# An fp32 transformer trunk on one core: a third K pair of the MLP's up projections as seven block products

## The chip, the cores and the metric

The kernel runs on one core of a Trainium2 chip. The metric is device time in microseconds, the median of three runs of the whole program.

## What is computed

A trunk of two decoder layers on 256 tokens of width 2048, all in float32: an attention of one kind in the first layer, of another in the second, and in each layer an MLP and a gated per-layer embedding. The change is in the MLP:

```python
hn = rmsnorm(h, mlp_norm_g[i])
h = h + jnp.square(jax.nn.relu(hn @ mlp_w1[i])) @ mlp_w2[i]
```

`mlp_w1[i]` is 2048 x 8192 and `mlp_w2[i]` 8192 x 2048, so that there are 33.6 million weights for the MLP of a layer, for 256 tokens.

## The kernel before

**The products.** A float32 matrix is used as two parts, a high one that TensorE's fp32r takes exactly and a low one, the rest. A product has three matmuls: high by high, low by high, high by low (`terms`). Weights come as chunks of 128 x 1024 floats: two K tiles (128 rows each) by 512 features. ScalarE copies a raw chunk to its high part (`copy`, L243, tile whi), VectorE subtracts to get the low one (`sub`, L251, wlo), and TensorE takes both. The features of 512 columns are called a quad. A quad over K = 2048 has eight chunks (K pairs), of 24 matmuls for a K pair of two quads, 12 for each chunk: two K tiles, two halves of the tokens (128 each), three matmuls. The tokens' part stands still in the array (`xa`, or `h` in the downs) and the weights stream through, 512 columns a matmul.

**The order of work.** `Program.run` goes through a list of chunks. At chunk n it emits the loads up to n + 7 as far as the four raw buffers allow, the copies up to n + 4, the splits up to n + 3, then one piece each of the work that goes on beside (generators, `advance`), and then the matmuls of chunk n. Each engine takes its instructions in the order in which they are emitted. There are six buffers for high parts and five for low ones.

**The MLP** (`mlp`) goes in four blocks of 2048 features. A block has four quads of ups (`up_plain`, `up_mixed`) and then four quads of downs over the same features (`downs`). The first two quads of a layer are plain. The other ups go in pairs of quads, seven in each layer: one pair in the first block, two in each of the other three. "First pair of a layer", "early pair" (right after the downs of the block before) and "late pair" (right after the early one) are used below.

**A pair** (`up_mixed`, `pair_major`) shares the chunks of two quads. Six of the eight K pairs are plain. The other two (MIXED = (2, 5)) are taken as a product of 2 x 2 blocks (tokens' halves by K tiles, K tiles by quads) in seven block products in place of eight, 21 matmuls for 24. For that VectorE makes two further weight chunks: t, a sum of the first quad's chunk a and a half of the second quad's chunk b (`make_t`, L531, tile ts), and u, two sums of half a chunk, written over b (`make_u`, L536 and L537). So a mixed K pair is a set of four chunks a, b, t and u with 6, 3, 6 and 6 matmuls, of which a, t and u are split in full and b by half. The raw chunk of a is held until u is made. The sums of the tokens' blocks, the forms (tile xf), are made once a layer by `x_forms`, after the two plain quads. The chunks stand in the order

```
first quad 0, 1 | set 2 | first quad 3, second quad 0, first quad 4 | set 5 | first quad 6, 7 | second quad 1, 3, 4, 6, 7
```

**What follows a pair.** After the last set four sums (`sums`, L778 to L783) make the common part of both quads' results; the banks' own part is added to it when a quad's last chunk is through (`done`, L790), ScalarE takes ReLU (L792) and square (L749), VectorE transposes blocks (L697), the rows go out to a DRAM tile (dU, L196) and come back turned, in four transfers (L200), and ScalarE and VectorE split them into high and low parts h (L757, L759), half a quad at a time. All this is spread over the chunks that come after. The second quad of a pair ends with the pair, so for an early pair it falls into the late pair, and for a late pair into the downs.

Of the kernel before, what the change touches and what calls it, by code (L numbers as in the profile page):

```python
# [10 lines left out]
F32 = mybir.dt.float32  # L11
F32R = mybir.dt.float32r
# [22 lines left out]
DMA_AHEAD = 7  # L35
SPLIT_AHEAD = 3
RAW_BUFS, HI_BUFS, LO_BUFS = 4, 6, 5
MIXED = (2, 5)

G_ATTN, G_MLP, G_PLE, G_KV, G_FIN = 0, 2, 4, 6, 7  # L40

# [1 line left out]
def f32(ap):  # L43
    return ap.bitcast(F32)
# [116 lines left out]
def kernel(ctx: ExitStack, tc: tile.TileContext, a: dict, out: bass.AP):  # L161
# [386 lines left out]
    def x_forms(k, gi, to):  # L548


        u = [tmp.tile([P, T], F32, tag="sq", name="sq", bufs=3) for _ in range(3)]
        for i in range(2):
            nc.scalar.activation(u[i], x[k + i], AF.Identity, scale=gain(gi, k + i))
        yield
        a, b, s = u
        nc.vector.tensor_sub(s[:, :P], a[:, P:], b[:, P:])
        nc.vector.tensor_sub(s[:, P:], a[:, :P], a[:, P:])
        nc.vector.tensor_sub(a[:, :P], a[:, :P], s[:, :P])
        nc.vector.tensor_sub(b[:, :P], b[:, :P], a[:, :P])
        f = cur["z"].tile([P, 2, 2 * T], F32R, tag="xf", name="xf", bufs=2)  # L560
        parts = ((slice(0, T), s), (slice(T, T + P), a[:, :P]), (slice(T + P, 2 * T), b[:, :P]))
        for c, v in parts:
            nc.scalar.copy(f[:, 0, c], v)
        yield
        for c, v in parts:
            nc.vector.tensor_sub(f[:, 1, c], v, f32(f[:, 0, c]))
        to[k // 2] = f
# [29 lines left out]
    def to_head(ps, norm, dst, roped, mark, late=0, lo=None):  # L597

        t = sum_halves(ps)
        for _ in range(1 + late):  # L600
            yield
        while norm.r is None:
            yield
        if callable(dst):
            dst = dst()
        elif dst is None:
            dst = t
        if not roped:
            nc.vector.tensor_mul(dst, t, norm.rb)
        else:  # L610
            sh = tmp.tile([32, T], F32, tag="rsh", name="rsh", bufs=2)
            nc.vector.stream_shuffle(sh, t[:32, :], ROPE_SWAP)
            nc.vector.tensor_mul(dst, t, norm.rc)
            nc.vector.tensor_mul(sh, sh, norm.rs)
            nc.vector.tensor_add(dst[:32, :], dst[:32, :], sh)
        if lo is not None:
            yield
            nc.scalar.copy(lo[0], dst)
            yield
            nc.vector.tensor_sub(lo[1], dst, f32(lo[0]))  # L620
        mark()
# [19 lines left out]
            out[-1].append(s)  # L641
        return out

    def taken_late(f, g, ops=()):

        both = [by_chunk(prog.collect(p)) for p in (f, g)]
        for c in range(0, KT // 2, 2):
            if c == KT // 2 - 2:
                for fn in ops:
                    prog.op(fn)  # L650
            for steps in both:
                prog.steps += steps[c] + steps[c + 1]

    def out_proj(src, nk, oT, gi, to, norm, hooks, twos, close):

# [70 lines left out]
    def mlp(layer, xg, norm, to, norm2, opening):  # L726
# [20 lines left out]
        def up(b, q, t):  # L747

            nc.scalar.activation(t, t, AF.Square)  # L749
            yield  # L750
            yield
            w = yield from turned(t, second if b == 0 and q == 1 else new)
            w4 = w.rearrange("p a (n i j r) -> p n a (i j) r", n=2, i=2, r=32)
            for n in range(2):
                h = cur["z"].tile([P, 2, 2, T], F32R, tag="h", name="h", bufs=8)
                h5 = h.rearrange("p c i (j a r) -> p c a (i j) r", j=2, r=32)
                nc.scalar.copy(h5[:, 0], w4[:, n])  # L757
                yield
                nc.vector.tensor_sub(h5[:, 1], w4[:, n], f32(h5[:, 0]))  # L759
                for i in range(2):  # L760
                    hid[b][4 * q + 2 * n + i] = (h[:, 0, i], h[:, 1, i])

        def up_plain(b, q, ps0, ps1, mm):

# [7 lines left out]
        def up_mixed(b, q):  # L772

            ts = []

            def sums(aux):
                s, o = row(), row()
                nc.scalar.copy(s[:, 0], aux["P1"])  # L778
                yield
                nc.vector.tensor_sub(s[:, 1], aux["R6"], s[:, 0])  # L780
                nc.vector.tensor_add(o[:, 0], aux["Q5"], s[:, 1])
                nc.vector.tensor_sub(s[:, 1], aux["Q7"], s[:, 1])
                nc.vector.tensor_sub(o[:, 1], o[:, 0], aux["Q7"])  # L783
                ts.extend((s, o))

            def done(i, ps):
                while not ts:
                    yield
                t = ts[i]
                nc.vector.tensor_add(t, ps, t)  # L790
                for j in range(2):
                    nc.scalar.activation(t[:, j], t[:, j], AF.Relu, scale=norm.col[:, j:j + 1])  # L792
                yield from up(b, q + i, t)

            plain_ = [c for c in range(KT // 2) if c not in MIXED]
            c0, c1, c2, c3, c4, c5 = plain_
            order = [(0, c0), (0, c1), MIXED[:1], (0, c2), (1, c0), (0, c3), MIXED[1:], (0, c4), (0, c5)] + \
                [(1, c) for c in plain_[1:]]
            pair_major(lambda i, c: a["w1"][layer * 128 + (b * 4 + q + i) * 8 + c], order, xg, forms, sums, done)

        def normed(k):
# [24 lines left out]
        def downs(b, q):  # L826
            token_major(chunks("w2", b, q), hid[b], lambda *ps: down(b, q, *ps), whole=True)

        taken_late(lambda: ups(0, 0, {4: [lambda: norm.factor(rows=True)]}), lambda: ups(0, 1), opening)
        def all_forms():  # L830
            for c in MIXED:
                yield from x_forms(2 * c, G_MLP + layer, forms)
                yield
        prog.op(all_forms)
        for b in range(NFB):
            for q in range(0, 4, 2):
                if b or q:
# [536 lines left out]
    def key_unit(n, i, which, at, hooks=None):  # L1374

        def done(ps0, ps1, mm):
# [3 lines left out]
            for g in range(GB):  # L1380
                while n_b1.r is None:
                    yield
                k4, c4, s4 = (v.rearrange("p (j a r) -> p j a r", j=2, a=4) for v in
                              (cur["E"].tile([P, T], F32, tag="et", name="et", bufs=7), n_b1.rc, n_b1.rs))
                src = w.rearrange("p a (g j r) -> p g j a r", j=2, r=32)[:, g]
                sh = tmp.tile([32, T], F32, tag="rsh", name="rsh", bufs=2)
                sh4 = sh.rearrange("p (j a r) -> p j a r", j=2, a=4)
                nc.vector.tensor_mul(k4, src, c4)
                nc.vector.stream_shuffle(sh4, src[:32], ROPE_SWAP)
                nc.vector.tensor_mul(sh4, sh4, s4)  # L1390
                nc.vector.tensor_add(k4[:32], k4[:32], sh4)
                yield
                t2 = k4.rearrange("p j a r -> p j (a r)")
                nc.scalar.copy(kt_blocks(g, 0, which), t2)
                yield
                nc.vector.tensor_sub(kt_blocks(g, 1, which), t2, f32(kt_blocks(g, 0, which)))
# [208 lines left out]

    def q_done(h, ps):
        t = sum_halves(ps)
        sh = tmp.tile([32, T], F32, tag="rsh", name="rsh", bufs=2)
        nc.vector.stream_shuffle(sh, t[:32, :], ROPE_SWAP)
        nc.vector.tensor_mul(t, t, n_b1.rc)  # L1610
        nc.vector.tensor_mul(sh, sh, n_b1.rs)
# [245 lines left out]
```

## Time and profile before

| | |
|---|---|
| Time, median of three runs | 2447.5 us (2447.45 to 2448.7) |
| Time of the profiled execution | 2447.25 us |
| Its span | 2445.5 us |
| Granted TensorE clock | 0.999 |
| TensorE, VectorE, ScalarE busy | 100%, 73%, 56% of the span |
| HBM | 217 GB/s over the span |

A busy time counts an engine's instructions, not how full they keep it; matmuls are pipelined. What ended an engine's idle time stands behind an arrow in the rows of the profile; "PE" is TensorE, "DVE" VectorE, "ACT" ScalarE, "SPq" the queue of SyncE, which issues the loads. Names are those of the program's tiles: mm and at are PSUM banks.

### The profile page before, as it was taken

How to read it: one execution, taken by the hardware profiler on the slowest of the kernel's cores; microseconds unless marked ns; L12 is line 12 of the kernel's file. 1: busy time of each engine (PE TensorE's matmuls, PEld its weight loads, DVE VectorE, ACT ScalarE, POOL GpSimd, SP SyncE). 2: the span in 40 equal slices, each digit the busy share in tenths (PEclk: the TensorE clock that was granted, in tenths of full speed). 3: DMA queues.
4: the chain of work that ended last, by engine and by line, in shares of the span. 5: the costliest groups of instructions: out<-in, count | busy, mean ns of one | idle time of the engine just before them, and what ended most of it. 6: DMA issues, size and time to landing. Idle time of an engine off the chain costs nothing.

```text
span 2445.5 us, 33009 instructions
## 1 busy us (share of the span) xinstructions
PE 2434.5 (100%) x11763; PEld 2050.8 (84%) x11763; DVE 1774.0 (73%) x2666; ACT 1371.5 (56%) x1997; POOL 10.3 (0%) x24
## 2 busy tenths in 40 slices
PE   9999999999999999999999999999999999999998
PEld 8888888888888888888888889988888888888887
DVE  7866687776585675777678989867658668567766
ACT  6544444565464454564564788756545546445556
POOL 0000000000000000000100000000000000000000
PEclk9999999999999999999999999999999999999999
DMA  7666665767577576687776743476857757758775
GB/s 276 201 214 215 196 210 197 223 222 249 182 240 235 190 250 220 194 271 241 243 242 210 256 165 121 141 226 219 262 182 233 240 186 239 233 187 257 247 233 161
DMA packets 174981, 532.26 MB, mean 218 GB/s; under 512 B 19616, under 2 KB 51808, under 8 KB 174816
## 3 DMA queue, kind: packets, MB, share of 16 engines
q1 hardware_dynamic: 173712, 528.30, 66.3%
q8 instruction: 92, 1.51, 0.2%
q0 software_dynamic: 528, 1.07, 0.1%
q10 hardware_dynamic: 576, 0.79, 0.1%
q14 instruction: 73, 0.60, 0.1%
HBM read 496.00 MB, written 34.08 MB: 217 GB/s over the span
## 4 chain that ended last, share of the span: by engine, by line
PE 99%; DVE 0%; DMA 0%; ACT 0%; SPq 0%; issue 0%; ACTq 0%; DVEq 0%
PE at L589 26%; PE mm L589 25%; PE at L493 21%; PE mm L384 11%; PE mm L386 6%; PE mm L493 3%; PE at L384 1%; PE at L386 1%; PE at L1682 1%; PE mm L1706 0%; PE mm L1446 0%; PE mm L916 0%; PE mm L918 0%; PE mm L917 0%; PE mm L1447 0%; PE at L1167 0%
## 5 line engine op out<-in xcount | busy, mean ns | idle before, releaser
L251 DVE TENSOR_TENSOR wlo<-raw,whi 128x1024 fp32r<-128x1024 f32 (+1 forms) x903 | 1075.8, 1199 | 500.3 <-PE mm L589 151.3
L243 ACT CAST whi<-raw 128x1024 fp32r<-128x1024 f32 (+1 forms) x903 | 930.5, 1039 | 727.2 <-PE mm L589 207.6
L493 PE MATMUL at<-whi,xa 128*128 128x512 f32 x1456 | 448.2, 389 | 0.0
L384 PE MATMUL mm<-xa,whi 128*128 128x512 f32 x1104 | 371.7, 395 | 0.0
L493 PEld LDWEIGHTS at<-whi,xa 128*128 128x128 f32 x1456 | 273.3, 188 | 56.8
L589 PE MATMUL mm<-whi,h 128*128 128x512 f32 x1024 | 315.2, 389 | 0.0
L589 PE MATMUL at<-whi,h 128*128 128x512 f32 x1024 | 315.2, 389 | 0.0
L493 PE MATMUL at<-wlo,xa 128*128 128x512 f32 x728 | 283.2, 389 | 0.0
L386 PE MATMUL mm<-xa,wlo 128*128 128x256 f32 x1104 | 273.3, 278 | 0.0
L589 PEld LDWEIGHTS at<-whi,h 128*128 128x128 f32 x1024 | 192.2, 188 | 39.9
L589 PEld LDWEIGHTS mm<-whi,h 128*128 128x128 f32 x1024 | 192.2, 188 | 39.9
L386 PEld LDWEIGHTS mm<-xa,wlo 128*128 128x128 f32 x1104 | 207.3, 188 | 18.0
L384 PEld LDWEIGHTS mm<-xa,whi 128*128 128x128 f32 x1104 | 193.3, 188 | 30.5 <-issue 0.4
L589 PE MATMUL at<-whi,xa 128*128 128x512 f32 x672 | 208.0, 391 | 1.5 <-DVE et L392 1.3
L589 PE MATMUL mm<-whi,xa 128*128 128x512 f32 x656 | 202.8, 390 | 0.0
L589 PE MATMUL mm<-wlo,h 128*128 128x512 f32 x512 | 199.2, 389 | 0.0
L589 PE MATMUL at<-wlo,h 128*128 128x512 f32 x512 | 199.2, 389 | 0.0
L493 PEld LDWEIGHTS at<-wlo,xa 128*128 128x128 f32 x728 | 136.6, 188 | 28.3
L589 PEld LDWEIGHTS at<-whi,xa 128*128 128x128 f32 x672 | 125.2, 189 | 26.9 <-issue 1.4
L589 PEld LDWEIGHTS mm<-whi,xa 128*128 128x128 f32 x656 | 122.5, 188 | 25.1
L589 PE MATMUL at<-wlo,xa 128*128 128x512 f32 x336 | 130.6, 390 | 0.2 <-DVE wlo L251 0.2
L589 PE MATMUL mm<-wlo,xa 128*128 128x512 f32 x328 | 127.7, 389 | 0.0
(405 smaller groups left out, 2698.5 us busy)
## 6 DMA issues: line engine op xcount, KB each, us to landing
raw<-in_w SPq DMA_DIRECT2D x512, 512.0 KB, 4.4
raw<-in_w_qk SPq DMA_DIRECT2D x96, 512.0 KB, 3.7
raw<-in_w_gate SPq DMA_DIRECT2D x64, 512.0 KB, 4.3
raw<-in_w_kv SPq DMA_DIRECT2D x48, 512.0 KB, 4.4
raw<-in_w_v SPq DMA_DIRECT2D x47, 512.0 KB, 4.4
dU<-z SPq DMA_DIRECT2D x46, 512.0 KB, 4.2
w<-dU SPq DMA_DIRECT2D x184, 128.0 KB, 5.0
raw<-in_w_q SPq DMA_DIRECT2D x32, 512.0 KB, 4.2
```

The lines of the kernel that those rows point to most:

```text
L243: nc.scalar.copy(hi[:, c], t[:, c])
L251: nc.vector.tensor_sub(lo[:, c], t[:, c], f32(hi)[:, c])
L384: nc.tensor.matmul(ps, hi[:, col:col + P], rhs, start=first, stop=False)
L386: nc.tensor.matmul(ps[:, :T], lo[:, col:col + P], rhs[:, :T], start=False, stop=last)
L493: nc.tensor.matmul(ps, x_, w_, start=b not in touched, stop=end and last[b] == n and i == 2)
L589: nc.tensor.matmul(st[j], *parts[j][i], start=k == i == 0, stop=k == kt - 1 and i == 2)
L1682: nc.tensor.transpose(tr[:, i * P:(i + 1) * P], src, ident)
```

## The change

MIXED becomes (1, 3, 5): three K pairs as sets, with a third buffer for forms. The order of a pair's chunks becomes

```
first quad 0, 2 | set 1 | first quad 4 | set 3 | first quad 6 | set 5 | first quad 7 | second quad 0, 2, 4, 6, 7
```

The layout of w1 in DRAM follows MIXED by itself. The forms are now made in the last plain chunks, before the second plain quad's last two (`mid` of `taken_late`). A quad's 512 features are split into h in one instruction each on ScalarE and VectorE, in place of two (lines L760 and L762 of the new kernel), with four buffers of four K tiles in place of eight of two. The small tile rsh of the rotary embedding moves from the pool tmp to the pool E, which is closed while the MLP runs.

```diff
-MIXED = (2, 5)
+MIXED = (1, 3, 5)
...
-        f = cur["z"].tile([P, 2, 2 * T], F32R, tag="xf", name="xf", bufs=2)
+        f = cur["z"].tile([P, 2, 2 * T], F32R, tag="xf", name="xf", bufs=len(MIXED))
...
-            sh = tmp.tile([32, T], F32, tag="rsh", name="rsh", bufs=2)
+            sh = cur["E"].tile([32, T], F32, tag="rsh", name="rsh", bufs=2)
...
-    def taken_late(f, g, ops=()):
+    def taken_late(f, g, ops=(), mid=()):
...
-            for steps in both:
+            for n, steps in enumerate(both):
                 prog.steps += steps[c] + steps[c + 1]
+                if c == KT // 2 - 2 and n == 0:
+                    for fn in mid:
+                        prog.op(fn)
...
-            w4 = w.rearrange("p a (n i j r) -> p n a (i j) r", n=2, i=2, r=32)
-            for n in range(2):
-                h = cur["z"].tile([P, 2, 2, T], F32R, tag="h", name="h", bufs=8)
-                h5 = h.rearrange("p c i (j a r) -> p c a (i j) r", j=2, r=32)
-                nc.scalar.copy(h5[:, 0], w4[:, n])
-                yield
-                nc.vector.tensor_sub(h5[:, 1], w4[:, n], f32(h5[:, 0]))
-                for i in range(2):
-                    hid[b][4 * q + 2 * n + i] = (h[:, 0, i], h[:, 1, i])
+            yield
+            w4 = w.rearrange("p a (i j r) -> p a (i j) r", j=2, r=32)
+            h = cur["z"].tile([P, 2, 4, T], F32R, tag="h", name="h", bufs=4)
+            h5 = h.rearrange("p c i (j a r) -> p c a (i j) r", j=2, r=32)
+            nc.scalar.copy(h5[:, 0], w4)
+            yield
+            nc.vector.tensor_sub(h5[:, 1], w4, f32(h5[:, 0]))
+            for i in range(4):
+                hid[b][4 * q + i] = (h[:, 0, i], h[:, 1, i])
...
-            order = [(0, c0), (0, c1), MIXED[:1], (0, c2), (1, c0), (0, c3), MIXED[1:], (0, c4), (0, c5)] + \
-                [(1, c) for c in plain_[1:]]
+            m0, m1, m2 = [(c,) for c in MIXED]
+            order = [(0, c0), (0, c1), m0, (0, c2), m1, (0, c3), m2, (0, c4)] + \
+                [(1, c) for c in (c0, c1, c2, c3, c4)]
...
-        prog.op(all_forms)
+        taken_late(lambda: ups(0, 0, {4: [lambda: norm.factor(rows=True)]}), lambda: ups(0, 1), opening,
+                   [all_forms])
```

VectorE in a late pair (the second pair of the third block), from the split of the first set's u to L537 of the second set, before:

```order
L251 TENSOR_TENSOR wlo_7682<-raw_7576,whi_7664 128x1024
L697 STREAM_TRANSPOSE z_7686<-t_7500 128x2x4x4x32
L251 TENSOR_TENSOR wlo_7702<-raw_7615,whi_7680 128x1024
L759 TENSOR_TENSOR h_7684<-w_7600,h_7684 128x4x4x32
L251 TENSOR_TENSOR wlo_7717<-raw_7633,whi_7700 128x1024
L759 TENSOR_TENSOR h_7705<-w_7600,h_7705 128x4x4x32
L251 TENSOR_TENSOR wlo_7730<-raw_7696,whi_7715 128x1024
L251 TENSOR_TENSOR wlo_7747<-raw_7698,whi_7728 128x1024
L531 TENSOR_TENSOR ts_7763<-raw_7698,raw_7713 128x1024
L251 TENSOR_TENSOR wlo_7767<-raw_7713,whi_7745 128x512
L536 TENSOR_TENSOR raw_7713<-ts_7763,raw_7698 128x512
L537 TENSOR_TENSOR raw_7713<-raw_7713 128x512
```

And from the same split in the kernel of the change (its L700, L762, L783 to L786 and L793 are L697, L759, L780 to L783 and L790 of before):

```order
L251 TENSOR_TENSOR wlo_7710<-raw_7604,whi_7692 128x1024
L700 STREAM_TRANSPOSE z_7712<-t_7546 128x2x4x4x32
L251 TENSOR_TENSOR wlo_7726<-raw_7643,whi_7708 128x1024
L251 TENSOR_TENSOR wlo_7740<-raw_7661,whi_7724 128x1024
L762 TENSOR_TENSOR h_7728<-w_7628,h_7728 128x4x8x32
L531 TENSOR_TENSOR ts_7753<-raw_7661,raw_7722 128x1024
L251 TENSOR_TENSOR wlo_7757<-raw_7722,whi_7738 128x512
L536 TENSOR_TENSOR raw_7722<-ts_7753,raw_7661 128x512
L537 TENSOR_TENSOR raw_7722<-raw_7722 128x512
L251 TENSOR_TENSOR wlo_7774<-ts_7753,whi_7755 128x1024
L251 TENSOR_TENSOR wlo_7790<-raw_7722,whi_7772 128x1024
L251 TENSOR_TENSOR wlo_7802<-raw_7736,whi_7788 128x1024
```

Before, three plain chunks are split between the sets, and two halves of h stand among them. In the change one plain chunk is split, the next set's a follows at once, and a whole quad's h stands ahead of the sum t.

VectorE at the end of the same pair, from the split of the first plain chunk behind the last set to those behind the first quad's add, before:

```order
L251 TENSOR_TENSOR wlo_7821<-raw_7743,whi_7804 128x1024
L251 TENSOR_TENSOR wlo_7830<-raw_7761,whi_7819 128x1024
L251 TENSOR_TENSOR wlo_7842<-raw_7815,whi_7828 128x1024
L251 TENSOR_TENSOR wlo_7854<-raw_7817,whi_7840 128x1024
L251 TENSOR_TENSOR wlo_7875<-raw_7826,whi_7852 128x1024
L780 TENSOR_TENSOR t_7856<-mm_7736,t_7856 128x512
L781 TENSOR_TENSOR t_7857<-mm_7720,t_7856 128x512
L782 TENSOR_TENSOR t_7856<-mm_7724,t_7856 128x512
L783 TENSOR_TENSOR t_7857<-t_7857,mm_7724 128x512
L251 TENSOR_TENSOR wlo_7897<-raw_7838,whi_7873 128x1024
L790 TENSOR_TENSOR t_7856<-at_7649,t_7856 128x1024
L251 TENSOR_TENSOR wlo_7919<-raw_7850,whi_7895 128x1024
```

And in the change, from the same split:

```order
L251 TENSOR_TENSOR wlo_7870<-raw_7809,whi_7854 128x1024
L251 TENSOR_TENSOR wlo_7879<-raw_7822,whi_7868 128x1024
L251 TENSOR_TENSOR wlo_7891<-raw_7864,whi_7877 128x1024
L251 TENSOR_TENSOR wlo_7903<-raw_7866,whi_7889 128x1024
L251 TENSOR_TENSOR wlo_7924<-raw_7875,whi_7901 128x1024
L783 TENSOR_TENSOR t_7905<-mm_7763,t_7905 128x512
L784 TENSOR_TENSOR t_7906<-mm_7743,t_7905 128x512
L785 TENSOR_TENSOR t_7905<-mm_7747,t_7905 128x512
L786 TENSOR_TENSOR t_7906<-t_7906,mm_7747 128x512
L793 TENSOR_TENSOR t_7905<-at_7677,t_7905 128x1024
L251 TENSOR_TENSOR wlo_7950<-raw_7887,whi_7922 128x1024
L251 TENSOR_TENSOR wlo_7968<-raw_7899,whi_7948 128x1024
```

The four sums of a pair stood one chunk ahead of the first quad's add, with its split between them. In the change they stand right ahead of it.

More of the change, by code (lines that the diff above doesn't have):

```diff
@@ L793, in done @@
                 yield from up(b, q + i, t)
-            plain_ = [c for c in range(KT // 2) if c not in MIXED]
-            c0, c1, c2, c3, c4, c5 = plain_
-            order = [(0, c0), (0, c1), MIXED[:1], (0, c2), (1, c0), (0, c3), MIXED[1:], (0, c4), (0, c5)] + \
-                [(1, c) for c in plain_[1:]]
+            c0, c1, c2, c3, c4 = [c for c in range(KT // 2) if c not in MIXED]
+            m0, m1, m2 = [(c,) for c in MIXED]
+            order = [(0, c0), (0, c1), m0, (0, c2), m1, (0, c3), m2, (0, c4)] + \
+                [(1, c) for c in (c0, c1, c2, c3, c4)]
             pair_major(lambda i, c: a["w1"][layer * 128 + (b * 4 + q + i) * 8 + c], order, xg, forms, sums, done)
@@ L827, in downs @@
             token_major(chunks("w2", b, q), hid[b], lambda *ps: down(b, q, *ps), whole=True)
-        taken_late(lambda: ups(0, 0, {4: [lambda: norm.factor(rows=True)]}), lambda: ups(0, 1), opening)
         def all_forms():
@@ L1385, in done @@
                 src = w.rearrange("p a (g j r) -> p g j a r", j=2, r=32)[:, g]
-                sh = tmp.tile([32, T], F32, tag="rsh", name="rsh", bufs=2)
+                sh = cur["E"].tile([32, T], F32, tag="rsh", name="rsh", bufs=2)
                 sh4 = sh.rearrange("p (j a r) -> p j a r", j=2, a=4)
@@ L1607, in q_done @@
         t = sum_halves(ps)
-        sh = tmp.tile([32, T], F32, tag="rsh", name="rsh", bufs=2)
+        sh = cur["E"].tile([32, T], F32, tag="rsh", name="rsh", bufs=2)
         nc.vector.stream_shuffle(sh, t[:32, :], ROPE_SWAP)
```

## The prediction

> **What bounds the kernel now.** I read the page first, then TensorE's waits, then one late pair of the MLP's ups: its path, its busy times, and VectorE's instructions in order of time. From the page, the span, the engines and the chain that ended last:
>
> ```profile
> span 2445.5 us, 33009 instructions
> PE 2434.5 (100%) x11763; PEld 2050.8 (84%) x11763; DVE 1774.0 (73%) x2666; ACT 1371.5 (56%) x1997; POOL 10.3 (0%) x24
> PE 99%; DVE 0%; DMA 0%; ACT 0%; SPq 0%; issue 0%; ACTq 0%; DVEq 0%
> ```
>
> TensorE ends the chain nearly everywhere. The waits of TensorE, all of them:
>
> ```profile
> PE at L589 <- DVE et L392: 1.3, 1, 1.3
> PE mm L1092 <- DVE ones L212: 1.1, 1, 1.1
> PE at L589 <- ACT whi L243: 0.2, 1, 0.2
> PE at L589 <- DVE wlo L251: 0.2, 1, 0.2
> ```
>
> They come to 2.8 us and none is in the ups. So a matmul less is worth its whole spacing, and a wait that is made new is paid in full. The first two rows below are pieces of the path in a late pair (the second pair of a block), start, length and count. The rows with two times and a colon are busy times from there: an early pair, then a late one.
>
> ```profile
> 871.39 8.84 PE at L493 x39
> 884.31 19.72 PE at L493 x87
> 819.71:861.90 42.19, 42.19 (x188) 34.94 (x187) 33.52 (x34) 22.58 (x24) 0.00 (x0) 1.00 0.63 213
> 861.90:904.03 42.13, 42.13 (x187) 34.88 (x187) 34.92 (x37) 25.94 (x30) 0.00 (x0) 1.00 0.72 229
> ```
>
> 19.72 over 87 is 0.2267 us a matmul. A pair has 186 of them by the code (six plain K pairs of 24, two mixed of 21), 42.2 us, which is the time that both windows show: no stall. The third busy time is VectorE's, 33.5 and 34.9 us of 42. It has 7 us to spare in a late pair, and that is what the change draws on.
>
> **The change, part by part.** *The matmuls.* A mixed K pair takes 21 instead of 24. One more in each of 14 pairs saves 14 x 3 = 42 matmuls, at 0.2267 us 9.5 us, all of it on the path. In the profiled execution (2447.25 us) that alone gives 2437.7.
>
> *What VectorE gets.* A mixed K pair has 3.5 splits of a full chunk where a plain one has 2, and a sum of a full chunk and two of half a chunk besides. These are VectorE's instructions around a late pair, with what ended the idle time before one in brackets:
>
> ```profile
> 849.07 1.22 DVE L790 TENSOR_TENSOR t<-at,t 128x1024 f32<-128x1024 f32 x1
> 853.79 1.23 DVE L251 TENSOR_TENSOR wlo<-raw,whi 128x1024 fp32r<-128x1024 f32 x1 [2.38 <-ACT whi L243]
> ...
> 859.47 0.68 DVE L251 TENSOR_TENSOR wlo<-raw,whi 128x512 fp32r<-128x512 f32 x1
> 861.91 1.22 DVE L790 TENSOR_TENSOR t<-at,t 128x1024 f32<-128x1024 f32 x1 [1.76 <-PE at L493]
> 863.05 0.68 DVE L536 TENSOR_TENSOR raw<-ts,raw 128x512 f32<-128x512 f32 x1
> 863.77 0.69 DVE L537 TENSOR_TENSOR raw<-raw 128x512 f32<-128x512 f32 x1
> 864.38 1.22 DVE L251 TENSOR_TENSOR wlo<-ts,whi 128x1024 fp32r<-128x1024 f32 x1
> 866.58 1.23 DVE L251 TENSOR_TENSOR wlo<-raw,whi 128x1024 fp32r<-128x1024 f32 x1 [0.98 <-ACT whi L243]
> 867.72 1.24 DVE L697 STREAM_TRANSPOSE z<-t 128x1024 f32<-128x1024 f32 x1
> 868.88 1.18 DVE L251 TENSOR_TENSOR wlo<-raw,whi 128x1024 fp32r<-128x1024 f32 x1
> ...
> 882.57 3.49 DVE L251 TENSOR_TENSOR wlo<-raw,whi 128x1024 fp32r<-128x1024 f32 x3
> ...
> 889.82 1.23 DVE L251 TENSOR_TENSOR wlo<-raw,whi 128x1024 fp32r<-128x1024 f32 x1 [1.87 <-ACT whi L243]
> 890.96 0.68 DVE L780 TENSOR_TENSOR t<-mm,t 128x512 f32<-128x512 f32 x1
> 893.61 1.22 DVE L251 TENSOR_TENSOR wlo<-raw,whi 128x1024 fp32r<-128x1024 f32 x1
> ```
>
> An instruction begins before the one ahead of it has ended, so work is counted by spacing: a full chunk 1.13 us (three splits in 3.49, of which the last lasts 1.22), half a chunk 0.61 (863.77 to 864.38), L536 with L537 1.33 (863.05 to 864.38), a transpose 1.16 (867.72 to 868.88). A mixed K pair more costs 1.5 x 1.13 + 1.13 + 1.33 = 4.2 us, so a late pair needs 34.9 + 4.2 = 39.1 us of VectorE in 41.5 us of TensorE. As a mean that fits. It is the place of the work that doesn't: three sets of block products now stand with one plain chunk between them, and VectorE can be ahead by its five buffers for low parts only.
>
> *TensorE's need in a late pair*, from the start of its first matmul: a plain chunk takes 12 x 0.2267 = 2.72 us, and the four chunks of a set 1.36, 0.68, 1.36 and 1.36. Two plain chunks, a set, one, a set, one, and a and b of the third set: its t begins at 22.44. Its third matmul is the first with a low part, so VectorE must have split t by 22.9 us.
>
> *VectorE's work up to there*, in the order of the change: from the add of the pair before (L790, now L793) to the split of the third t there are 13 instructions on a full chunk's width (that add, eight splits, two sums t, two splits of h), so 14.7 us; a transpose, 1.16; two half chunks, 1.2; three L536 with L537, 4.0; the last split, 1.2. Together 22.3. The 0.98 us of row 866.58 stays, because ScalarE still has the ReLU and square of that add ahead of the copy of u: 23.3. A quad's split in one go is in this: 1.13 where two halves took 2 x 0.61, a gain of 0.1 for each.
>
> *When it can begin.* Before, VectorE waited 1.76 us at 861.91 for TensorE; this cover goes. The stretch from the first quad's add (849.07) to the end of the half split (859.47 + 0.68 = 860.15) takes 11.1 us. In the change the four sums stand right ahead of that add, 890.96 to 893.61 = 2.65 us, and the first quad's last matmul is five chunks, 13.6 us, before the pair's end. If VectorE is free then, it ends 11.1 + 2.7 - 13.6 = 0.2 us after the pair's start. If the split ahead of the sums is late by as much as at 889.82 (1.87, behind a copy that waited), 2.1 us. I take 1.2, about the middle, since the loads behind the third set come as late here as behind the second set there.
>
> So the third t is split at 1.2 + 23.3 = 24.5 against 22.9: **a stall of 1.6 us in a late pair**, between 0.6 (begin at 0.2) and 2.5 (begin at 2.1). Part of it falls at the second t: the same count gives 15.7 there against 15.0 + 0.45. Six late pairs (three blocks in two layers) make 9.6 us.
>
> *Early pairs after downs.* Instead of the add they have one of y (the same length), and neither transpose nor h: 1.16 + 2 x 1.13 + 0.98 less, with nothing late at the start. Their third t is ready 4 us early or more: no stall.
>
> *The first pair of a layer* follows two plain quads and still makes the forms of x:
>
> ```profile
> 526.51 0.28 DVE L556 TENSOR_TENSOR sq<-sq 128x128 f32<-128x128 f32 x1
> ...
> 527.57 1.22 DVE L251 TENSOR_TENSOR wlo<-raw,whi 128x1024 fp32r<-128x1024 f32 x1
> 528.70 0.82 DVE L566 TENSOR_TENSOR xf<-sq,xf 128x256 fp32r<-128x256 f32 x3
> 529.44 2.35 DVE L251 TENSOR_TENSOR wlo<-raw,whi 128x1024 fp32r<-128x1024 f32 x2
> ```
>
> A set costs 1.06 (L556 to L559) and 0.74 (L566). One of the three is now made in the last plain chunks, where VectorE idles; two stay ahead of the third t. From L536 of the first set, which begins about with the pair: 12 full chunks 13.6, a transpose 1.2, two halves 1.2, three L536 with L537 4.0, the forms 3.6, the last split 1.2 make 24.8 against 22.9. That is a stall of 1.9; twice 3.8 us, with 1 us either way for each.
>
> *The rest.* The h buffers hold the same features, the third form is bought with the room of rsh, whose helpers now take it from pool E; no instruction outside the MLP moves. Nothing for both.
>
> **Sum:** -9.5 + 9.6 + 3.8 = +3.9 us. With 2447.25 that is 2451.2; the median of the runs is 0.25 us above the profiled execution, so I give 2451.3. By the ends it is -9.5 + 6 x 0.6 + 2 x 0.9 = -4.1 (2443.4) and -9.5 + 6 x 2.5 + 2 x 2.9 = +11.3 (2458.8). A measurement of this kernel can tell about 0.2%, 4.9 us, from no change, so the forecast is: none that can be told.
>
> **The rivals.** *VectorE keeps up.* The whole saving, 2438.0. For it: 39.1 of 41.5 us as a mean, and no stall on VectorE in the ups today. Against it: the count leaves 0.6 us even from the early start, unless the 0.98 us goes.
>
> *The third set's second chunk comes late.* There are four buffers for raw chunks, and a set holds two of them. The load of b of the third set waits for L536 of the second set, by the count at 1.2 + 12.7 = 13.9 us; its sum t comes at 20.2. That leaves 6.3 us. The transfers in the late pair, with the median us to landing:
>
> ```profile
> raw<-in_w SPq DMA_DIRECT2D x17, 512.0 KB, 4.9
> dU<-z SPq DMA_DIRECT2D x2, 512.0 KB, 4.0
> ```
>
> It decides from 6.3 us on, 1.4 above the median; and SyncE's queue has the way back of the second quad's features ahead of it, which waits for its dU (issued at the transpose's end, 8.1, landed at 12.1) and issues four transfers before that load. At 1.1 us more in each of the eight pairs: 2451.3 + 8.8 = 2460. For it: the sum t of the second set waited for such a load today, if briefly:
>
> ```profile
> 875.03 1.22 DVE L531 TENSOR_TENSOR ts<-raw 128x1024 f32<-128x1024 f32 x1 [0.36 <-DMA raw<-in_w]
> ```
>
> Against it: the 1.4 us of leeway, which grows by what VectorE is late.
>
> *VectorE's instructions don't overlap.* If each took its whole duration, 1.22 for 1.13 and 0.68 for 0.61, a pair's count grows by 13 x 0.09 + 6 x 0.05 = 1.5 us: 2451.3 + 8 x 1.5 = 2463. Row 882.57 speaks against it, three in 3.49 and not 3.66. The Trainium skill (VectorE: DVE Perf Modes, "The TRN2 errata — SBUF-src ops pay a fixed extra latency per instruction") has (N + 151)/0.96 ns for an fp32 tensor_tensor, 1224 for N = 1024, and says that the latency lies between instructions. As a duration the trace agrees (1.22); as a spacing it doesn't, and the sum goes by the spacing.
>
> That the change doesn't do what it says can nearly be ruled out: the new order has 2562 matmuls at L493 where 2604 stood.
>
> **How the numbers follow.** My count has a chance of 0.69, its own range 2443.4 to 2458.8: 0.52 of it lies within 0.2% (2442.6 to 2452.4) and 0.17 above, where a stall is over 1.8 us. VectorE keeps up, with small stalls left or none: 0.15, faster. The late load: 0.12, slower. No overlap: 0.04, slower. So faster 0.15, same 0.52, slower 0.33. The range from 2442 to 2460 takes in my count and the late load, and leaves out 0.15 + 0.04.
>
> **What would show it.** Right: in TensorE's waits, rows of L493 on VectorE's wlo, 1 to 2 us at the third t of each late pair and each first pair, and none in early pairs; VectorE without idle time from the add at the late pair's start to the third t, but for about 1 us behind ScalarE; a late pair of 41.5 + 1.6 us, an early one of 41.5. Wrong: late pairs of 41.5 us (VectorE keeps up), stalls in early pairs too, waits of L531 on raw of a microsecond or more (the late load), or time lost outside the ups.

## The result and the profile after

The changed kernel takes 2460.5 us (median of 4 runs, 2458.96 to 2464.09) where the kernel before takes 2448.1 (median of 4, 2447.45 to 2448.76): a ratio of 1.0053, 95% interval 1.0035 to 1.0070. It is slower by half a per cent, 9.2 us above the forecast of 2451.3 and half a microsecond above the range; the forecast was "none that can be told". The profiled execution took 2459.28 us. Its span, engines and chain, from the page:

```profile
span 2457.5 us, 33053 instructions
PE 2431.2 (99%) x11721; PEld 2041.1 (83%) x11721; DVE 1830.0 (74%) x2718; ACT 1382.1 (56%) x2003; POOL 10.3 (0%) x24
PE 93%; DVE 3%; DMA 2%; issue 1%; ACT 1%; SPq 0%; ACTq 0%; DVEq 0%
```

TensorE has 42 matmuls fewer, as said (11763 - 11721), and the chain now leaves it: 3% of the span by VectorE, 2% by transfers, where before it was TensorE's for 99%. The waits of TensorE after, engine and line that waits, what it waits for, us in total, times, the longest:

```profile
PE mm L493 <- DVE wlo L251: 14.1, 14, 1.2
PE at L589 <- DVE et L392: 1.3, 1, 1.3
PE at L493 <- DVE wlo L251: 1.1, 3, 0.6
PE mm L1095 <- DVE ones L212: 1.1, 1, 1.1
PE at L589 <- ACT whi L243: 0.3, 1, 0.3
```

The first and third row are new: 17 waits of the ups' matmuls for a low part, 15.2 us. The rest stood there before. Where they lie is read from the busy times of an early pair, then a late one, in the same block as those shown of before (window; us, then PE, PEld, VectorE, ScalarE, GpSimd, the granted clock, the DMA's share, GB/s):

```profile
822.59:864.08 41.49, 41.49 (x185) 34.36 (x184) 35.94 (x38) 22.55 (x25) 0.00 (x0) 1.00 0.57 190
864.08:907.83 43.75, 42.09 (x185) 34.18 (x183) 37.70 (x39) 27.11 (x31) 0.00 (x0) 1.00 0.74 229
```

The early pair takes 41.49 us with TensorE busy throughout: 0.7 less than before, the whole saving and no stall. The late one takes 43.75 and is busy for 42.09. Over all six late pairs the stall is 2.70, 2.28, 3.78, 2.87, 2.50 and 2.63 us, 16.8 together; the two first pairs of a layer take 43.69 and 43.85, a stall of 2.20 and 2.37. The downs between take 87.04 us as before, and outside the ups the two executions differ by 0.2 us in all. So -9.5 + 16.8 + 4.6 = +11.9, and the profiled executions differ by 12.0.

VectorE around this late pair, which starts at 864.08 (start, us, line, operation; in brackets what ended the idle time before):

```profile
850.79 1.23 DVE L251 TENSOR_TENSOR wlo<-raw,whi 128x1024 fp32r<-128x1024 f32 x1 [0.80 <-ACT whi L243]
...
854.58 1.22 DVE L793 TENSOR_TENSOR t<-at,t 128x1024 f32<-128x1024 f32 x1
...
865.57 1.22 DVE L793 TENSOR_TENSOR t<-at,t 128x1024 f32<-128x1024 f32 x1
...
870.23 1.23 DVE L251 TENSOR_TENSOR wlo<-raw,whi 128x1024 fp32r<-128x1024 f32 x1 [0.98 <-ACT whi L243]
...
883.63 1.22 DVE L762 TENSOR_TENSOR h<-w,h 128x1024 fp32r<-128x1024 f32 x1
884.77 1.22 DVE L531 TENSOR_TENSOR ts<-raw 128x1024 f32<-128x1024 f32 x1
...
887.83 1.22 DVE L251 TENSOR_TENSOR wlo<-ts,whi 128x1024 fp32r<-128x1024 f32 x1
```

The second quad's add begins at 865.57, 1.49 us after the pair's start; from there to the end of the third t's split (887.83 + 1.22 = 889.05) VectorE is idle once, the 0.98 us behind ScalarE. The third t is ready 24.97 us after the pair's start, and 22.9 were needed. TensorE at the same places:

```profile
879.03 0.61 PE L493 MATMUL mm<-whi,xf 128*128 128x512 f32 x2
880.24 0.50 PE L493 MATMUL mm<-wlo,xf 128*128 128x512 f32 x1 [0.60 <-DVE wlo L251]
880.58 0.62 PE L493 MATMUL mm<-whi,xf 128*128 128x512 f32 x2
...
887.41 0.63 PE L493 MATMUL mm<-whi,xf 128*128 128x512 f32 x2
889.11 0.50 PE L493 MATMUL mm<-wlo,xf 128*128 128x512 f32 x1 [1.06 <-DVE wlo L251]
889.44 0.63 PE L493 MATMUL mm<-whi,xf 128*128 128x512 f32 x2
```

Two matmuls start at 879.03, so the third was due 0.45 later, at 879.48; it starts at 880.24, 0.76 late, of which the row shows 0.60 as a wait (the idle time is counted from the modelled end of the matmul ahead, 0.16 after the next could start). And the one behind it starts 0.34 later, not 0.2267: a stall costs another 0.11 on restart. That is why 15.2 us of waits cost 21.4 us: 17 times 0.27 is 4.6, and the other 1.6 lie in delays too short to be listed. At the second t 0.87 us are lost in this pair, at the third 1.34.

### The profile page after: what moved, and what is told of

Same layout as the page of the kernel before. It is cut to its first block, busy times and chain, and to the rows that moved or that the text cites. A ratio compares the mean times of both kernels' runs of the same rounds, so it can differ in the third digit from the quotient of the medians.

```text
span 2457.5 us, 33053 instructions
## 1 busy us (share of the span) xinstructions
PE 2431.2 (99%) x11721; PEld 2041.1 (83%) x11721; DVE 1830.0 (74%) x2718; ACT 1382.1 (56%) x2003; POOL 10.3 (0%) x24
## 4 chain that ended last, share of the span: by engine, by line
PE 93%; DVE 3%; DMA 2%; issue 1%; ACT 1%; SPq 0%; ACTq 0%; DVEq 0%
PE at L589 26%; PE mm L589 25%; PE at L493 15%; PE mm L384 11%; PE mm L386 6%; PE mm L493 3%; DVE wlo L251 1%; PE at L384 1%; DMA w<-dU 1%; PE at L386 1%; PE at L1685 1%; DMA y<-dU 0%; DMA raw<-in_w 0%; ACT whi L243 0%; PE mm L1709 0%
## 5 line engine op out<-in xcount | busy, mean ns | idle before, releaser
L493 PE MATMUL at<-whi,xa 128*128 128x512 f32 x1288 | 396.6, 389 | 0.0
L493 PEld LDWEIGHTS at<-whi,xa 128*128 128x128 f32 x1288 | 241.8, 188 | 50.3
L493 PE MATMUL at<-wlo,xa 128*128 128x512 f32 x644 | 250.9, 390 | 1.1 <-DVE wlo L251 1.1
L589 PE MATMUL at<-whi,xa 128*128 128x512 f32 x672 | 207.8, 391 | 1.6 <-DVE et L392 1.3
L589 PEld LDWEIGHTS at<-whi,xa 128*128 128x128 f32 x672 | 124.9, 188 | 27.3 <-issue 1.4
L493 PEld LDWEIGHTS at<-wlo,xa 128*128 128x128 f32 x644 | 120.9, 188 | 27.3 <-DVE wlo L251 2.3
L589 PE MATMUL at<-wlo,xa 128*128 128x512 f32 x336 | 130.7, 390 | 0.1
```

The source lines that it names most:

```text
L493: nc.tensor.matmul(ps, x_, w_, start=b not in touched, stop=end and last[b] == n and i == 2)
L589: nc.tensor.matmul(st[j], *parts[j][i], start=k == i == 0, stop=k == kt - 1 and i == 2)
```

## The experiments

Theory: VectorE's work ahead of the third t makes the stalls, as the prediction's count has it, and they are larger because VectorE starts later. The rivals are those that each expectation names. Times are medians, and ratios are to runs of the kernel before on the same chip (2448.0, 2448.6 and 2448.4 us in the three groups, e1 to e4, e5 to e8, e9 to e12). The change itself was timed only for the result, so a difference to it is one across these groups. In the diffs a `yield` lets one chunk more go ahead of what follows it.

**e1, work held behind the third t.** In late pairs the second quad's transpose and the first quad's split of h are held back.

```
             yield
             yield
+            for _ in range(11 if b and q == 1 else 0):
+                yield
             w = yield from turned(t, second if b == 0 and q == 1 else new)
             yield
+            for _ in range(9 if b and q == 0 else 0):
+                yield
```

> Of the change, with one thing moved: the transpose of an early pair's second quad waits eleven chunks longer, and the splits of h of its first quad nine, so that neither stands ahead of the third set's t in the late pair. The work is the same. Theory Q (VectorE's queue: the third t is late because VectorE has 23.5 us of work up to it, from a start 1.75 us after the pair's): 3.4 us less work stands ahead of the third t, which is then in time. Late pairs take 41.5 us, the 16.8 us of stalls in the six go, and the first pairs of the layers keep theirs (4.6 us): 2460.5 - 16.8 = 2443.7, within 2442 to 2446. Rival L (the raw chunk of b is late): the loads of b stay where they were in the order of raw chunks; the time stays at 2457 to 2461, but for what the way back of the features, which moves too, had in it.

2443.99 us, ratio 0.9983 (0.9973 to 0.9992). Five of the stretches of two pairs take 82.96 to 82.98 us, which is no stall, and one 83.24; the first pairs, left as they were, 43.84 and 44.69. The waits of the ups in its trace:

```profile
PE mm L493 <- DVE wlo L251: 2.7, 3, 1.2
PE at L493 <- DVE wlo L251: 0.8, 2, 0.5
```

VectorE in a late pair of it that starts at 861.50, from the third set on:

```profile
863.21 1.22 DVE L797 TENSOR_TENSOR t<-at,t 128x1024 f32<-128x1024 f32 x1
...
882.08 1.22 DVE L251 TENSOR_TENSOR wlo<-ts,whi 128x1024 fp32r<-128x1024 f32 x1
...
885.64 1.22 DVE L766 TENSOR_TENSOR h<-w,h 128x1024 fp32r<-128x1024 f32 x1
886.77 1.24 DVE L700 STREAM_TRANSPOSE z<-t 128x1024 f32<-128x1024 f32 x1
```

The add (now L797) begins as late as in the change, 1.71 us after the pair's start. The third t is split at 883.30, 21.80 us after it, 3.2 earlier than in the change, and that is the transpose and the two splits of h (1.16 + 2 x 1.13 = 3.4), which stand behind it now. VectorE has the same work, for 37.45 us of this pair where it was 37.70 in the change (the second quad's split of h begins 0.7 us behind the pair's end); its order takes away 16.5 of the 16.8 us. The way back and ScalarE's copies of h move with it, so e1 alone can't put it all down to VectorE; e2 adds work to VectorE and to nothing else.

**e2, the split of h done twice in late pairs.**

```
             nc.vector.tensor_sub(h5[:, 1], w4, f32(h5[:, 0]))
+            if b and q < 2:
+                nc.vector.tensor_sub(h5[:, 1], w4, f32(h5[:, 0]))
```

> Of the change, with each of VectorE's splits of h of an early pair done twice over (the same result written again): two more instructions of 1.13 us ahead of the third t in each late pair, and none in the loads or on another engine. Theory Q: 2.26 us more stall in each of the six late pairs, 13.6 us in all, 2474, within 2470 to 2476. Rival L: the added work lies in time that VectorE spends waiting; 0 to 2 us, at most 2463.

2474.55 us, 1.0105 (1.0090 to 1.0120). The six stretches take 529.2 us together against 514.5 in the change, 2.45 us a pair, where two more instructions are 2 x 1.13 = 2.26 by the prediction's spacing and 2.5 in the trace (from the add to the third t VectorE takes 25.99 us there, 23.48 in most late pairs of the change). With no slack left, what VectorE gets ahead of the third t comes out at TensorE one for one. With e1 this shows that a late pair's stall is VectorE's work ahead of the third t. (Two of the six have a stretch of lower clock, see the last section; it lies ahead of the third t, which TensorE would have waited for all the same: 88.27 and 88.67 us, the other four 87.95 to 88.33.)

**e3 and e4, one more raw buffer.** The fifth raw buffer is paid for with a high-part buffer; both kernels give that up, and e3 alone gets the raw buffer for it.

```
-RAW_BUFS, HI_BUFS, LO_BUFS = 4, 6, 5
+RAW_BUFS, HI_BUFS, LO_BUFS = 5, 5, 5
```

(e4: 4, 5, 5)

> Of the change, with five raw buffers instead of four, paid for with one of the six buffers of high parts. To be read against the run with five high buffers and four raw ones. Theory Q with the late start put down to loads behind the third set: the sums and the first quad's add begin up to 1.75 us earlier, and the pair with five raw buffers is 1 to 1.75 us faster for each of the six late pairs than its partner, 6 to 10 us. If the start hangs on the order of the sums alone (TensorE's end of the quad), the two are alike to 2 us. Against the change itself 2455 to 2462.

> Of the change, with five buffers for high parts instead of six and nothing else: the partner of the run with five raw buffers. ScalarE can copy a chunk only when TensorE is through with the one five before it, a chunk later than now. Theory Q: stalls grow by 0.5 to 1 us for each late pair and by as much for the first ones, 2463 to 2469. Without an effect of ScalarE's lead: 2460.5.

2466.09 us, 1.0073 (1.0058 to 1.0088), and 2480.42 us, 1.0130 (1.0113 to 1.0147). Both lie above what was expected. The high-part buffer was mis-sized: giving it up costs 20 us and not 3 to 9. In the profiled executions 8 to 9 of them lie outside the ups, in both kernels. The other part tells something. The six stretches take 512.6 us in e3 and 524.3 in e4 (514.5 in the change): the raw buffer is worth 11.7 us there, 10.0 without what a lower clock took (the last section), where 6 to 10 were expected. VectorE's add in e4, in a late pair that starts at 867.35, and the chunk ahead of the first quad's sums:

```profile
855.44 1.22 DVE L251 TENSOR_TENSOR wlo<-raw,whi 128x1024 fp32r<-128x1024 f32 x1 [1.40 <-ACT whi L243]
...
870.21 1.22 DVE L793 TENSOR_TENSOR t<-at,t 128x1024 f32<-128x1024 f32 x1
```

and in e3, in one that starts at 865.15:

```profile
850.90 1.22 DVE L251 TENSOR_TENSOR wlo<-raw,whi 128x1024 fp32r<-128x1024 f32 x1 [0.33 <-ACT whi L243]
...
865.67 1.22 DVE L793 TENSOR_TENSOR t<-at,t 128x1024 f32<-128x1024 f32 x1
```

The add begins 2.86 us after the start in e4, 1.49 in the change (0.80 waited at the same chunk), 0.52 in e3. ScalarE's copy of that chunk waited for a raw load in e4 (1.58 us) and in the change:

```profile
849.71 1.05 ACT L243 CAST whi<-raw 128x1024 fp32r<-128x1024 f32 x1 [0.98 <-DMA raw<-in_w]
```

In e3 it waited for its load too (1.25 us), but came earlier, 15.33 us ahead of the late pair's start, where e4 has 12.98 and the change 14.37. So, with five high-part buffers at least, the loads behind the third set, which wait for a raw buffer, set when VectorE begins, as the prediction's two bounds supposed.

**e5, the same held in the first pairs too, and the forms made earlier.**

```
+            for _ in range(11 if q == 1 else 12 if b == q == 0 else 0):
+                yield
             w = yield from turned(t, second if b == 0 and q == 1 else new)
             yield
+            for _ in range(9 if b and q == 0 else 0):
+                yield
...
-        taken_late(lambda: ups(0, 0, {4: [lambda: norm.factor(rows=True)]}), lambda: ups(0, 1), opening,
-                   [all_forms])
+        taken_late(lambda: ups(0, 0, {4: [lambda: norm.factor(rows=True)]}), lambda: ups(0, 1), opening + [all_forms])
```

> The holding of the first run, carried over to the first pair of a layer: the transposes of the two plain quads wait as well until the third set's t is split, and the forms of x are made two chunks earlier, before the last chunks of both plain quads. Theory Q: no stall in the ups at all, so that the 42 matmuls saved show in full: 2448.0 - 9.5 = 2438.5, within 2437.5 to 2441, and pairs of 41.5 us everywhere. Rival (the saving is lost elsewhere too: the held work falls on the downs or on the next pair's sums): 2442 to 2446, with stalls at new places.

2442.55 us (2439.16 to 2444.00), 0.9971 (0.9961 to 0.9982), 4 us above what was expected. No wait of more than 0.2 us for wlo is left in the ups; one first pair takes 41.48, the other 43.20, of which 1.7 us is not in the ups: the first downs wait for the h that was held:

```profile
PE mm L589 <- ACT h L764: 1.6, 1, 1.6
PE mm L589 <- DVE h L766: 1.3, 2, 0.9
```

Work held for too long is missed by the next reader: part of the stall moved, as the rival had it.

**e6, the forms made earlier, nothing held** (the last part of e5's diff alone).

> Of the change, with the forms of x made two chunks earlier and nothing else: more of the forms' 1.8 us a set is out of the way when the first pair of a layer begins. Theory Q: the first pairs' stalls, 2.2 and 2.4 us, fall by one set of forms, 1.0 to 1.8 us each, and the late pairs keep theirs: 2460.5 - 3 = 2457.5, within 2456 to 2459. Rival (the first pairs stall for their transposes' way or the loads): 2460 to 2461.

2461.25 us, 1.0052 (1.0039 to 1.0066), against 2460.49: no gain where 3 us were expected. The first pairs take 43.83 and 46.06 (1.7 of the last is a lower clock, see the last section). With the forms first, the first set's own work comes later: its L536 starts 1.0 us after the start of layer 1's first pair where it started 0.2 after in the change, and the third t is ready no sooner.

**e7, two plain chunks between the sets.** The first quad then ends three chunks ahead and not five.

```
-            order = [(0, c0), (0, c1), m0, (0, c2), m1, (0, c3), m2, (0, c4)] + \
-                [(1, c) for c in (c0, c1, c2, c3, c4)]
+            order = [(0, c0), (0, c1), m0, (0, c2), (1, c0), m1, (0, c3), (1, c1), m2, (0, c4)] + \
+                [(1, c) for c in (c2, c3, c4)]
```

> Of the change, with two plain chunks between the sets instead of one (the second quad's first two chunks stand there), so that the first quad ends three chunks ahead and not five. Theory Q: ahead of the third t TensorE has 5.4 us more and VectorE 2.3 us more, which is 3.2 us of relief, more than the 2.8 us of stall in a late pair; but the add, ReLU and square of the first quad and what follows them come 5.4 us nearer to the pair's end, so that VectorE begins the late pair later and part of the stall comes back at the first set: 1 to 2.5 us for each late pair, none in the first pairs, 2448.0 - 9.5 + 6 to 15 = 2445 to 2453. Rival (spacing of the sets alone decides): 2438.5 to 2441.

2465.65 us, 1.0067 (1.0053 to 1.0081): worse than the change, where a gain was expected. The first pairs gain (42.11 and 41.48), the late ones lose. VectorE's two adds at a late pair that starts at 866.44:

```profile
861.16 1.22 DVE L793 TENSOR_TENSOR t<-at,t 128x1024 f32<-128x1024 f32 x1
...
869.87 1.22 DVE L793 TENSOR_TENSOR t<-at,t 128x1024 f32<-128x1024 f32 x1
```

The first quad's add comes 5.3 us before the pair's start (9.5 in the pair shown of the change) and the second's 3.4 after it (1.5). That the sets lie further apart doesn't make up for it: the stalls spread over all three sets. Waits of the ups and of the downs:

```profile
PE mm L493 <- DVE wlo L251: 7.3, 12, 1.1
PE at L493 <- DVE wlo L251: 5.1, 10, 0.6
PE mm L589 <- DVE h L762: 2.4, 3, 0.8
PE at L493 <- ACT whi L243: 1.1, 1, 1.1
```

**e8, the features split in two halves again**, as in the kernel before, at their old place, ScalarE's first copy right behind the way back:

```
             w = yield from turned(t, second if b == 0 and q == 1 else new)
-            yield
-            w4 = w.rearrange("p a (i j r) -> p a (i j) r", j=2, r=32)
-            h = cur["z"].tile([P, 2, 4, T], F32R, tag="h", name="h", bufs=4)
...
+            w4 = w.rearrange("p a (n i j r) -> p n a (i j) r", n=2, i=2, r=32)
+            for n in range(2):
+                h = cur["z"].tile([P, 2, 2, T], F32R, tag="h", name="h", bufs=8)
...
+                nc.scalar.copy(h5[:, 0], w4[:, n])
+                yield
+                nc.vector.tensor_sub(h5[:, 1], w4[:, n], f32(h5[:, 0]))
```

> Of the change, with a quad's h again split in two halves of two K tiles each, as before, and eight small buffers. Theory Q: VectorE's spacing is 2 x 0.61 for 1.13, 0.1 us more for each of two splits ahead of the third t, and the halves come in four places instead of two, so 0.2 to 0.6 us for each late pair: 2460.5 + 1 to 4 = 2461.5 to 2464.5. Without an effect of the split in one go: 2460.5, within 1.

2471.45 us, 1.0088 (1.0072 to 1.0103): 11 us over the change, where 1 to 4 were expected. Two things differ from the change, halves and place. e10 to e12 take them apart.

**e10, the split in one go alone, on the kernel before** (the diff of e8 turned round, made to the kernel before).

> The kernel before, with one part of the change alone: a quad's features split in one go, one step later, in four h buffers. The prediction's term: 0.1 us of VectorE less for each quad, where VectorE isn't waited for: 2447.5 to 2448.6, the same as before. Rival (fewer, larger instructions free both engines for more than that, and before had hidden waits): under 2446.

2447.81 us, 1.0000 (0.9991 to 1.0009). Nothing, as the prediction had it.

**e11, the change without the step ahead of the split.**

```
             w = yield from turned(t, second if b == 0 and q == 1 else new)
-            yield
             w4 = w.rearrange("p a (i j r) -> p a (i j) r", j=2, r=32)
```

> The change, with the split in one go left as it is, but without the step that it puts ahead of it: ScalarE's copy of the features stands one chunk earlier, as in the kernel before. Theory place (in the run with two halves, ScalarE and VectorE stood idle for up to 2 us behind a way back of the features that had not landed; the step more is what lets it land): stretches of two pairs 1 to 4 us longer than the change's, as with the two halves, 2466 to 2472. Theory halves (the two smaller instructions of each engine cost it): as the change, 2459 to 2462.

**e12, two halves, with the step ahead kept** (e8's diff, but the first `yield` stays).

> The change, with the features split in two halves again, but with the step ahead of them kept. Theory place: the way back lands before the first copy, so only the ledger's 0.1 us a half and the second half's later place are added: 2460.5 to 2463.5. Theory halves: as the run with two halves at the earlier place, 2469 to 2473.

2468.56 us, 1.0084 (1.0070 to 1.0098), and 2462.89, 1.0060 (1.0047 to 1.0074). So with the step 2460.5 in one go and 2462.9 in halves; without it 2468.6 and 2471.5. The place is worth 8 to 9 us, the halves 2 to 3, about what a lower clock took in the two kernels with halves (3.4 us in each profile, the last section; e12's two executions with a granted clock of 0.999 took 2461.0 and 2461.8). ScalarE in a late pair of e11 that starts at 2047.90, then VectorE:

```profile
2066.95 1.05 ACT L759 CAST h<-w 128x1024 fp32r<-128x1024 f32 x1 [1.58 <-DMA w<-dU]
```

```profile
2068.03 1.23 DVE L761 TENSOR_TENSOR h<-w,h 128x1024 fp32r<-128x1024 f32 x1 [1.22 <-ACT h L759]
...
2073.37 1.22 DVE L251 TENSOR_TENSOR wlo<-ts,whi 128x1024 fp32r<-128x1024 f32 x1
```

ScalarE stands for 1.58 us at the copy of the second quad's features until they have landed, VectorE for 1.22 at the split behind it, and the third t is ready 26.69 us after the pair's start. In the same pair of the change one chunk more goes ahead of that copy:

```profile
2061.62 1.05 ACT L760 CAST h<-w 128x1024 fp32r<-128x1024 f32 x1 [0.24 <-DMA w<-dU]
```

0.24 us, and VectorE doesn't stand at all. In this change the step that looks idle is what keeps the way back off VectorE's path.

**e9, less held in the first pairs.** From e1 and e5 together: the late pairs as in e1, in block 0 only the splits of h, for a few chunks.

```
+            for _ in range(11 if b and q == 1 else 0):
+                yield
             w = yield from turned(t, second if b == 0 and q == 1 else new)
             yield
+            for _ in range(9 if b and q == 0 else 5 if b == q == 0 else 4 if b == 0 and q == 1 else 0):
+                yield
```

> The change, with the second quad's transpose held for 11 steps in the late pairs (b over 0), the first quad's way back split 9 steps later there, and in block 0 the split of the hidden features held less than when every pair was held at once: 5 steps for the first quad and 4 for the second of the first pair. Theory (VectorE's work ahead of the third t, nothing else, makes the stall; holding it costs only where the downs come to need it): no wait of L493 of over 0.5 us in late pairs or first pairs and none of L589 on h, 84 us less stall: 2438.5, 2437.5 to 2441. Rival (holding moves the lateness to the downs whatever the number of steps, as in the run that held all): waits of L589 on h of 1 us or more stay, 2442 to 2445.

2441.33 us (2440.85 to 2441.59), 0.9971 (0.9960 to 0.9982): 7 us under the kernel before and faster than the change by 19. All waits of TensorE in its trace:

```profile
PE at L589 <- DVE et L392: 1.2, 1, 1.2
PE mm L1099 <- DVE ones L212: 1.1, 1, 1.1
PE at L493 <- DVE wlo L251: 1.0, 2, 0.5
PE at L589 <- DVE wlo L251: 0.4, 1, 0.4
```

No wait for h in the downs, so the rival falls. The time lies 0.3 us above the range given. The first pairs take 42.36 and 42.28, three of the stretches 0.3 us over 82.96; these 2.7 us in all are what it is above the expected 2438.5. (The "84 us less stall" in the expectation is a slip: 2460.5 - 2438.5 is 22.) It is the best version here; its difference to e5 is within the spread of e5's runs.

## Why the prediction was wrong

**The matmuls, -9.5 us:** right. An early pair takes 41.49 us, where 41.5 was given.

**VectorE's work from the add to the third t, 23.3 us:** right to 0.2. In the late pairs at 649.89, 822.59, 2001.67 and 2174.17 (the starts of their stretches) it takes 23.48. In that of 1828.80 it is 23.64, and in that of 994.87 24.79: there the way back of the second quad's features isn't in time. ScalarE in this pair:

```profile
1056.30 1.05 ACT L760 CAST h<-w 128x1024 fp32r<-128x1024 f32 x1 [1.09 <-DMA w<-dU]
```

and VectorE stands 0.92 us for that copy. The prediction weighed the way back only as something ahead of a load on SyncE's queue, not as something that the split of h waits for.

**When it can begin, 1.2 us after the pair's start:** this is the step that failed first, and with 6 x 0.55 = 3.3 us the largest part of the error. The bounds were 0.2 and 2.1, and the middle was taken; it is 1.49 to 1.94, 1.75 in the mean. "The loads behind the third set come as late here as behind the second set there" was the reason for the middle, and it speaks for the upper end: the bound of 2.1 was made from just such a copy that waited. e3 and e4 speak for those loads as what sets it.

**"A stall of 1.6 us in a late pair":** 2.8. The sum by the parts: 0.55 later (1.75 for 1.2), 0.18 in the count, 0.22 for two restarts of 0.11, which the prediction didn't price at all, makes 0.95 for each of the six pairs, 5.7 us; and 1.3 and 0.2 us more in the two pairs with a longer count. That is 7.2, and 9.6 + 7.2 = 16.8, as measured. "A wait that is made new is paid in full" was too little: 15.2 us of waits cost 21.4. For the pair of 822.59: 1.49 + 23.48 - 22.9 + 0.21 = 2.28.

**The first pair of a layer, 1.9 us:** 2.20 and 2.37. VectorE in that of layer 1, which starts at 1697.90:

```profile
1698.09 0.65 DVE L536 TENSOR_TENSOR raw<-ts,raw 128x512 f32<-128x512 f32 x1
...
1721.72 1.22 DVE L251 TENSOR_TENSOR wlo<-ts,whi 128x1024 fp32r<-128x1024 f32 x1
```

The count of 24.8 us from L536 on is right: 1698.09 to 1722.94 is 24.85. But L536 begins 0.2 after the pair's start, and again there are two restarts. The two pairs make 4.6 us for 3.8. With the 7.2 us of the late pairs and the 0.2 outside the ups, these are the 8 us by which the profiled execution lies above the sum's 2451.2. The rest of the 9.2 is that the runs' median lies 1.2 us above the profiled execution, where 0.25 was taken.

**Early pairs, none:** right.

**The rest, nothing:** right, 0.2 us outside the ups, and for the split in one go on the kernel before (e10). In the change the split's new place is worth 8 us (e11), but the prediction's count had it at that place, with no wait behind the way back; so the sum isn't wrong by it. What was missed is how near the wait was.

**The rivals.** VectorE keeps up: no, as the change stands; as e1 and e9 order its work, yes. The late load of the third set's second chunk: no L531 waited for a load in the late pairs of the trace above, and the 2460 that it gave is reached by another road. No overlap: the spacing stayed at 1.14 us (883.63 to 884.77). As the forecast's own upper end (2458.8) was made from a begin at 2.1 and no restart, it lay below what came.

The chances were wrong with it: 0.52 on "within 0.2%" rested on a stall of no more than 1.8 us, and every one of the six was over it.

## What to carry to other kernels

Count an engine's work up to the first result that is waited for, not over the whole stage: here 39 of 41.5 us, by the count, fit as a mean, and the stall was 2.8 us; the same work in another order had none. Where the count's start depends on something that itself waits for a buffer, take the late bound, and add to each stall what the restart costs. When an in-order engine has work that nobody needs soon (here a transpose and the split of h), let it stand behind what is needed next, but not so long that its own reader comes.

## What the runs showed of the hardware

**Waiting that falls into one window of 3.41 us can halve TensorE's clock.** In e8, after a late pair's stalls, busy time in windows of 2 us (the clock is the third figure from the right):

```profile
1065.00:1067.00 2.00, 1.24 (x3) 0.48 (x3) 1.97 (x3) 1.12 (x2) 0.00 (x0) 1.00 0.21 29
1067.00:1069.00 2.00, 1.49 (x5) 1.26 (x6) 1.95 (x3) 2.00 (x3) 0.00 (x0) 0.84 0.61 238
1069.00:1071.00 2.00, 2.00 (x6) 1.52 (x6) 2.00 (x3) 1.32 (x2) 0.00 (x0) 0.50 0.54 154
1071.00:1073.00 2.00, 2.00 (x9) 1.59 (x8) 1.14 (x2) 0.64 (x1) 0.00 (x0) 0.81 0.94 297
```

TensorE was busy for 2.7 of 4 us, no single wait was over 1.2 us, and then the granted clock was 0.50 for about 3.4 us: 0.16 + 0.50 + 0.19 of windows of 2 us is 1.7 us of lost clock. The traces of e2, e4, e8 and e12 have two such stretches of 1.7 us, those of e1, e3, e5, e6 and e7 one, those of the kernel before, of the change, of e9, of e10 and of e11 none, apart from the last 5 to 9 us of every trace. In e8 they are 3.4 of the 12.6 us between its span and the change's. Executions of one kernel differ in it: of the change's four, that of 2464.09 us has a granted clock of 0.997 and the others 0.999. The Trainium skill (TensorE: Matmul & The Clock Gate, "Part 1: The HAM clock gate (the "warmup" mystery)") has the clock at one half after one or more idle windows of about 3.4 us. The half clock and its length agree with the trace; that the whole window must be idle doesn't. In the change a late pair has even less work in as long a time, with the clock at 1.00:

```profile
1060.00:1062.00 2.00, 1.24 (x3) 0.48 (x3) 1.97 (x4) 1.12 (x2) 0.00 (x0) 1.00 0.06 10
1062.00:1064.00 2.00, 1.14 (x5) 0.95 (x6) 1.95 (x2) 2.00 (x3) 0.00 (x0) 1.00 0.67 252
```

What tells the two apart can be read from the traces' clock. In each of the nine traces that have such stretches, their starts and that of the one at the trace's end lie whole multiples of 3.4133 us apart: in e8 they are at 1068.34, 2078.69 and 2464.39, which is 296 and 113 times that. So the clock goes by windows on a fixed grid. In e8 the window ahead of the fall runs from 1064.93, and TensorE is busy for 2.07 of its 3.41 us. In the change the least busy one in a pair runs from 1060.52 and has 2.18, since the waiting is shared between it and the one before. Over all traces, the eleven windows of ups ahead of a fall are busy for 1.42 to 2.07 us, and every other one of ups at the full clock for 2.08 or more. The busy time isn't the measure itself, though: five windows outside the ups, in which 12 to 16 matmuls begin (3 to 7 in the eleven), are busy for 1.80 to 1.98 us, and no fall follows. Against the span's start the grid lies elsewhere in nearly every trace, so it is luck which stall falls into one window.

**A high-part buffer is worth 20 us** in this kernel (e4 against the change). In the profiled executions, 20.7 us apart, some 8 lie outside the MLP's ups and 3.4 are lost clock.
